# The end of a one-layer encoder step: the last 256 columns of y turned to token rows by TensorE, the upper columns scaled by GpSimd

## The chip, the cores and the metric

The kernel runs on one core of a Trainium2 chip. A core has TensorE (PE, with its weight loads as PEld), VectorE (DVE), ScalarE (ACT), GpSimd (POOL) and SyncE (SP, here only a queue that issues DMAs). The metric is the device time of one launch in microseconds (us); lower is better. The time before is 2154.39 us, the median of three runs from 2150.38 to 2154.47.

## The reference, cut to what matters

The reference is one inference step of a one-layer streaming encoder over 1024 prompt tokens and 64 sample tokens, width 1024: retention and sliding-window attention, a mix, cross attention and a SwiGLU, each added to the residual. Only the last two lines concern the change: the SwiGLU's down projection completes the residual stream, and the final RMSNorm scales every token by its own factor and every feature by a gain.

```python
    return (jax.nn.silu(hn @ w_gate) * (hn @ w_up)) @ w_down
...
    y = xf * lax.rsqrt(jnp.mean(xf * xf, axis=-1, keepdims=True) + EPS)
    if g is not None:
        y = y * g.astype(jnp.float32)
...
    y_prompt = rms_norm(hp, g_final)
    y_sample = rms_norm(hs, g_final)
```

## The kernel before, in words

Activations lie transposed: features on the 128 partitions, the 1088 tokens as columns. The residual y is eight tiles `y[0]` to `y[7]` of 128 features by 1088 columns; in the profile `y[0]` is called `rstd_f`, the others `y`. Matrix products run in a split of each operand into a high and a low part (three matmuls in place of one: `mm3`, lines 157 to 159), and most of the kernel in a Strassen-like scheme (`strassen`, with `multiply` at lines 223, 224 and 226).

The down projection goes over three groups of features of the hidden layer. In the last group the upper half of the columns, 544 to 1087 (`c = 2` below), is completed by the Strassen products, and the function `finish` completes the lower 544 columns by 16 plain products: eight (one for each `y[m]`) for columns 0 to 271 (`c = 0`), then eight for columns 272 to 543 (`c = 1`). A product is nine matmuls. Each is followed by `grow`: VectorE adds the product from PSUM to `y[m]` (line 1746) and ScalarE squares the sum (line 1750). `gather` adds a square to the running sum of squares in `rstd` on VectorE (line 1755).

For each of the three column groups the norm then takes these steps. `sums`: TensorE multiplies 128-token pieces of `rstd` with a matrix of ones, so that token sums land with tokens on partitions (line 1764). `roots`: six small steps give one factor per token (lines 1861 to 1868; the square root on ScalarE, the rest on VectorE). `spread`: TensorE multiplies the factors, broadcast, with the identity, so that each partition holds the factor of every column (line 1782), and ScalarE copies it to `rstd` (line 1786). `scale`: VectorE multiplies `y[m]` by gain and factor in one operation (line 1792) and a DMA stores it; some tiles get the gain by ScalarE (`gain`, line 1797) and the factor by GpSimd (`aside`, line 1805).

PSUM has eight banks, held as four pairs (`bank_pair`, pool `pst` with four buffers). In `finish` the helper `bank` takes a whole pair for each use and leaves its second half idle.

The order on each engine is set by a scheduler of the tile framework, which tracks which instruction reads and writes which tile and puts semaphore waits into the program. `in_order` holds a TensorE step behind the TensorE step before it, and `queued` does the same for VectorE steps in `finish`, so that there the written order stands.

Of the kernel before, what the change touches and what calls it, by code (L numbers as in the profile page):

```python
# [11 lines left out]
F32 = mybir.dt.float32  # L12
F32R = mybir.dt.float32r
AF = mybir.ActivationFunctionType
ALU = mybir.AluOpType
# [4 lines left out]
P = 128  # L20
D = 1024
# [19 lines left out]
HALF = T // 2  # L41
HC = HALF // 2
OPS = ("B11", "T1", "T2", "B21", "T3", "B22", "T4", "B12")

# [65 lines left out]
class Kernel:  # L110
# [1616 lines left out]
    def finish(self, y, rest):  # L1727


        nc = self.nc  # L1730
        tt, stt, ts = nc.vector.tensor_tensor, nc.vector.scalar_tensor_tensor, nc.vector.tensor_scalar
        cols = [slice(0, HC), slice(HC, HALF), slice(HALF, T)]
        squares, factors = {}, {}
        bank = lambda: self.bank_pair()[:, 0, :]

        def product(c, m, q, xs):
            ps = bank()[:, :HC]
            for k, x in enumerate(xs):
                ks = slice(k * P, (k + 1) * P)
                x = x.rearrange("p a (b c) -> p a b c", b=2)[:, :, c]  # L1740
                self.mm3(ps, q[:, 0, ks], q[:, 1, ks], x[:, 0], x[:, 1], k == 0, k == len(xs) - 1)
            return ps

        def grow(c, m, ps):
            v = y[m][:, cols[c]]
            self.queued(lambda: tt(out=v, in0=ps, in1=v, op=ALU.add))
            sq = self.rstd[:, cols[c]]
            if m:
                sq = self.hl.tile([P, HALF], F32, tag="hl", name="sq")[:, :HC]
            nc.scalar.activation(sq, v, AF.Square)  # L1750
            squares[c, m] = sq
# [4 lines left out]

        def sums(c, *more):

            spans = self.spans(cols[c].stop - cols[c].start)
            ps = bank()[:, :2 * len(spans)].rearrange("p (t two) -> p t two", two=2)  # L1760
            parts = [self.rstd[:, cols[c]], *more]
            steps = [(x, i, a, w) for x in parts for i, (a, w) in enumerate(spans)]
            for j, (x, i, a, w) in enumerate(steps):
                self.last_mm = nc.tensor.matmul(ps[:, i, :], x[:, a:a + w], self.ones[:, :2], start=j == 0,  # L1764
                                                stop=j == len(steps) - 1).ins
            r = self.np.tile([P, 5], F32, tag="rf", bufs=2, name="rs_f")[:, :len(spans)]
            factors[c] = r, spans, ps[:, :, 0]

        def roots(c, between=None):
            r, spans, ps = factors[c]  # L1770
            v = self.np.tile([P, 5], F32, tag="vf", bufs=2, name="rf_v")[:, :len(spans)]
            t = self.np.tile([P, 5], F32, tag="tf", bufs=2, name="rf_t")[:, :len(spans)]
            self.steps(r, v, t, ps, between)

        def spread(c, copied=True):
            r, spans, _ = factors[c]
            for part in ((0, 2), (2, 5)) if len(spans) > 4 else ((0, len(spans)),):
                pb = bank()
                a0, a1 = spans[part[0]][0], spans[part[1] - 1][0] + P
                for i in range(*part):  # L1780
                    at = spans[i][0] - a0
                    self.last_mm = nc.tensor.matmul(pb[:, at:at + P], r[:, i:i + 1].broadcast_to([P, P]), self.ident,  # L1782
                                                    start=True, stop=True).ins
                c0 = cols[c].start
                if copied:
                    self.last_copy = nc.scalar.copy(self.rstd[:, c0 + a0:c0 + a1], pb[:, :a1 - a0]).ins
            return pb

        def scale(c, k, by=None, queue=nc.sync):
            o = y[k][:, cols[c]]  # L1790
            by = self.rstd[:, cols[c]] if by is None else by
            self.queued(lambda: stt(o, o, self.gains[:, 3, k:k + 1], by, ALU.mult, ALU.mult))
            queue.dma_start(self.io["o_y"][k, :, cols[c]], o)

        def gain(c, k):
            o = y[k][:, cols[c]]
            nc.scalar.mul(o, o, self.gains[:, 3, k:k + 1])

        def put(c, k, queue=nc.sync):
            queue.dma_start(self.io["o_y"][k, :, cols[c]], y[k][:, cols[c]])  # L1800

        def aside(c, k, queue=None):
            o = y[k][:, cols[c]]
            with self.tc.issue_after(self.last_aside) if self.last_aside else nullcontext():
                self.last_aside = nc.gpsimd.tensor_tensor(out=o, in0=o, in1=self.rstd[:, cols[c]], op=ALU.mult).ins
            if queue:
                put(c, k, queue)

        self.last_aside = None
        left = (5, 6, 7)  # L1810
        spare = (5, 6)
        for j in range(2 * KT):
            c, m = divmod(j, KT)
            ps = self.in_order(lambda: product(c, *rest[m]))
            grow(c, rest[m][0], ps)
            if (j - 1) % KT and j and j < 2 * KT - 1:
                gather((j - 1) // KT, rest[(j - 1) % KT][0])
# [8 lines left out]
            if j == KT + 6:  # L1826
                pb0 = self.in_order(lambda: spread(0))[:, :HC]
                aside(0, KT - 1, nc.sync)
            if c and m in (0, 1, 2, 5, 6):
                scale(2, m if m < 3 else m - 2)  # L1830
            if c and 0 < m < 4:
                gain(2, left[m - 1])
            if c and m == 4:
                gain(0, KT - 1)
        for k in spare:
            gain(1, k)
        for k in range(3):
            scale(0, k, pb0)
        for k in left:
            aside(2, k)  # L1840
        self.in_order(lambda: sums(1, *(squares[1, rest[i][0]] for i in (KT - 2, KT - 1))))
        roots(1, lambda: scale(0, 3, pb0))
        for k in range(4, KT - 1):
            scale(0, k, pb0)
            if k < KT - 2:
                put(2, left[k - 4])
        pb = self.in_order(lambda: spread(1))[:, :HC]
        queues = [nc.sync, nc.scalar]
        for i, k in enumerate((0, 1, 2, 5, 3, 4, 6, 7)):
            if i == 3:  # L1850
                with self.tc.issue_after(self.last_copy):
                    put(2, left[2], nc.scalar)
            if k in spare:
                aside(1, k, queues[i % 2])
            else:
                scale(1, k, pb, queues[i % 2])

# [81 lines left out]
```

## Time and profile before

| what | us |
|---|---|
| runs | 2150.38, 2154.39, 2154.47 |
| span of the profiled execution | 2150.0 |
| TensorE busy | 2130.1 |
| VectorE busy | 1550.7 |
| ScalarE busy | 875.7 |
| GpSimd busy | 536.5 |
| first product of `finish` starts | 2114.70 |
| last product of `finish` ends | 2136.64 |
| last store issued | 2146.17 |

The page gives no time of the profiled execution beside its span; the span lies 0.38 us under the lowest run and 4.39 us under the median. Times in the profile are us from the span's start. Matmuls are pipelined: one of 272 columns is listed with 0.29 us, but starts 0.13 us after the one before it. One fp32 matmul that isn't split by the kernel is listed as two instructions. "DVE rstd_f" and "DVE y" in the chain of waits are VectorE steps that write `y`.

### The profile page before, as it was taken

To read this page: it belongs to the slowest core of one execution; us is meant where nothing else is said; L and a number is where in the kernel's file an instruction comes from. 1 tells how busy PE (TensorE), PEld (TensorE's weight loads), DVE (VectorE), ACT (ScalarE), POOL (GpSimd) and SP (SyncE) were. 2 spreads that over 40 slices of the span, in tenths; PEclk is the share of its full clock that TensorE was granted. 3 is DMA by queue.
4 is the path that set the end of the run, shared out by engine and by line. 5 is a ranking of instruction groups with operands and counts; after the bars stand their busy time and mean duration, and the time that the engine had idled before them with its cause. 6 is when DMAs were issued, how large, how long until landed. Compare 5 with 4: busy or idle time off the path is not lost. (4 is left out here: it accounts for less than half of the span.)

```text
span 2150.0 us, 41711 instructions
## 1 busy us (share of the span) xinstructions
PE 2130.1 (99%) x16377; PEld 2080.0 (97%) x16377; DVE 1550.7 (72%) x2909; ACT 875.7 (41%) x1897; POOL 536.5 (25%) x450
## 2 busy tenths in 40 slices
PE   9999999999999999999999999999999999999998
PEld 9999999999999997889999999999999999999998
DVE  8987979776677568656545555778777777877688
ACT  7343434344434356553233433333222222344344
POOL 0000000012253125540000000015556555514532
PEclk9999999999999999999999999999999999999999
DMA  7344444434345485336443121422342333383442
GB/s 257 126 133 120 129 136 128 139 119 155 121 144 176 159 265 188 116 115 212 137 143 104 40 63 53 155 65 98 121 146 94 106 113 106 103 328 125 141 131 99
DMA packets 169893, 290.85 MB, mean 135 GB/s; under 512 B 39266, under 2 KB 96546, under 8 KB 169698
## 3 DMA queue, kind: packets, MB, share of 16 engines
q1 hardware_dynamic: 161522, 268.74, 38.8%
q0 software_dynamic: 3424, 10.82, 1.4%
q10 hardware_dynamic: 4752, 8.64, 1.1%
q8 instruction: 129, 2.11, 0.4%
q14 instruction: 66, 0.54, 0.1%
HBM read 196.97 MB, written 91.16 MB: 134 GB/s over the span
## 5 line engine op out<-in xcount | busy, mean ns | idle before, releaser
L125 DVE TENSOR_TENSOR wq<-raw,wq 128x512 fp32r<-128x512 f32 (+1 forms) x499 | 429.6, 866 | 145.1 <-ACT wq L124 141.9
L124 ACT CAST wq<-raw 128x512 fp32r<-128x512 f32 (+1 forms) x499 | 301.6, 614 | 556.0 <-PE pq L226 217.8
L224 PE MATMUL pq<-T,wq 128*128 128x272 f32 x1832 | 492.1, 288 | 0.5 <-DVE T L125 0.5
L223 PE MATMUL pq<-T,wq 128*128 128x272 f32 x1832 | 490.2, 287 | 2.0 <-ACT wq L124 1.1
L224 PE MATMUL pq<-B,wq 128*128 128x272 f32 x1592 | 427.2, 288 | 1.0 <-DVE B L125 1.0
L223 PE MATMUL pq<-B,wq 128*128 128x272 f32 x1592 | 425.6, 287 | 0.8 <-ACT B L124 0.8
L226 PE MATMUL pq<-T,wq 128*128 128x272 f32 x1832 | 382.7, 289 | 1.0 <-DVE wq L125 1.0
L201 POOL TENSOR_TENSOR raw<-raw 128x512 f32<-128x512 f32 (+1 forms) x44 | 64.3, 1461 | 1252.2 <-DVE wq L125 569.6
L223 PEld LDWEIGHTS pq<-T,wq 128*128 128x128 f32 x1832 | 344.2, 188 | 3.2 <-ACT xsq L502 1.3
L224 PEld LDWEIGHTS pq<-T,wq 128*128 128x128 f32 x1832 | 344.0, 188 | 1.5 <-issue 0.7
L226 PE MATMUL pq<-B,wq 128*128 128x272 f32 x1592 | 331.9, 289 | 0.0
L224 PEld LDWEIGHTS pq<-B,wq 128*128 128x128 f32 x1592 | 299.0, 188 | 2.4 <-DVE B L125 1.9
L223 PEld LDWEIGHTS pq<-B,wq 128*128 128x128 f32 x1592 | 298.9, 188 | 1.1 <-ACT B L124 1.0
L226 PEld LDWEIGHTS pq<-T,wq 128*128 128x128 f32 x1832 | 289.7, 189 | 2.4 <-DVE wq L125 1.2
L226 PEld LDWEIGHTS pq<-B,wq 128*128 128x128 f32 x1592 | 251.7, 189 | 0.9 <-issue 0.7
L277 DVE TENSOR_TENSOR u<-pq,u 128x544 f32<-128x544 f32 x177 | 127.3, 720 | 69.4 <-PE pq L226 69.0
L616 DVE TENSOR_TENSOR stage<-pq,u 128x544 f32<-128x544 f32 x112 | 80.4, 720 | 32.2 <-PE pq L226 26.0
L157 PE MATMUL pd<-xc,wq 128*128 128x256 f32 (+1 forms) x256 | 74.6, 292 | 0.0
L159 PE MATMUL pd<-xc,wq 128*128 128x256 f32 (+1 forms) x256 | 74.3, 290 | 0.0
L158 PE MATMUL pd<-xc,wq 128*128 128x256 f32 (+1 forms) x256 | 74.1, 290 | 0.0
L1566 POOL TENSOR_TENSOR stage<-stage,rstd_f 128x544 f32<-128x544 f32 x40 | 63.9, 1607 | 39.1 <-ACT stage L1565 39.1
L204 POOL TENSOR_TENSOR raw<-raw 128x512 f32<-128x512 f32 (+1 forms) x44 | 59.4, 1349 | 52.8 <-DVE wq L125 50.3
(388 smaller groups left out, 4515.3 us busy)
## 6 DMA issues: line engine op xcount, KB each, us to landing
hl<-d_op SPq DMA_DIRECT2D x85, 272.0 KB, 5.4
d_qkv<-stage SPq DMA_DIRECT2D x44, 272.0 KB, 2.5
d_op<-stage SPq DMA_DIRECT2D x44, 272.0 KB, 2.4
d_op<-ht SPq DMA_DIRECT2D x44, 272.0 KB, 3.2
raw<-w_gate SPq DMA_DIRECT2D x22, 512.0 KB, 3.5
raw<-w_up SPq DMA_DIRECT2D x22, 512.0 KB, 4.5
raw<-w_down SPq DMA_DIRECT2D x16, 512.0 KB, 4.6
d_gate<-stage ACTq DMA_DIRECT2D x28, 272.0 KB, 2.7
```

Source lines behind the costliest of these rows:

```text
L124: self.last_cast = self.nc.scalar.copy(hi, src).ins
L125: return self.nc.vector.tensor_tensor(out=lo, in0=src, in1=hi.bitcast(F32), op=ALU.subtract).ins
L157: mm(ps, wh, xh, start=start, stop=False)
L158: mm(ps, wh, xl, start=False, stop=False)
L159: self.last_mm = mm(ps, wl, xh, start=False, stop=stop).ins
L201: tt(out=a11, in0=a11, in1=a21, op=sub)
L223: mm(ps[:, c, :HC], w[:, 0, ks], x[:, 0, cs], start=start, stop=False)
L224: mm(ps[:, c, :HC], w[:, 0, ks], x[:, 1, cs], start=False, stop=False)
L226: self.last_mm = mm(ps[:, c, :HC], w[:, 1, ks], x[:, 0, c * HC:(c + 1) * HC], start=False, stop=stop).ins
L277: add = lambda out, a, b: nc.vector.tensor_tensor(out=out, in0=a, in1=b, op=ALU.add)
L616: nc.vector.tensor_tensor(out=o, in0=ps, in1=sb, op=ALU.add)
L1566: nc.gpsimd.tensor_tensor(out=g, in0=g, in1=r[t], op=ALU.mult)
```

## The change: what it does

The lower columns are cut at 288 in place of 272: `c = 0` is columns 0 to 287, `c = 1` columns 288 to 543 (256 of them). The products and their adds are as before, with 288 and 256 columns.

For `c = 1` there is no `spread` and no scaling along columns. TensorE turns 128-token blocks of `y[m]`: `turn` multiplies the block, as the stationary operand, with a diagonal matrix of the gains (`diag`, eight 128x128 pieces that ScalarE makes from the identity), so that tokens come to lie on partitions with the gain already in. Sixteen such fp32 matmuls fill two PSUM pairs. Then the factor is a scalar for each partition, and four operations of 128x512 (two on VectorE, two on ScalarE) write the result, which is stored in a new output `o_yt`, token by token; the host puts it in its place in y. The sums of `c = 1` are taken in four parts, between the turns.

For `c = 2` ScalarE multiplies five tiles by the gain during the first products (or earlier: the scheduler moves four of them ahead), and GpSimd multiplies these five by the factor right after the `spread` that follows product 5; VectorE scales the other three between later products. For `c = 0` two tiles go the same way by GpSimd, and six by VectorE. `sums` and `roots` of `c = 2` come after product 3 in place of product 5, and its `spread` after product 5 in place of product 7.

`bank` now hands out both halves of a PSUM pair before it takes the next pair.

```diff
+CUT = 288
...
-        cols = [slice(0, HC), slice(HC, HALF), slice(HALF, T)]
-        bank = lambda: self.bank_pair()[:, 0, :]
+        cols = [slice(0, CUT), slice(CUT, HALF), slice(HALF, T)]
+        ring, slots = self.slots["T2"]
+        extra = [self.rings[ring].tile(f"last{i}", F32, slot=s).rearrange("p a n -> p (a n)") for i, s in enumerate(slots)]
+        diag = extra[0][:, :KT * P].rearrange("p (k m) -> p k m", m=P)
+        turned = extra[1][:, :2 * D].rearrange("p (i m) -> p i m", i=2)
+
+        def bank():
+            if not banks:
+                pair = self.bank_pair()
+                banks.extend((pair[:, 0, :], pair[:, 1, :]))
+            return banks.pop(0)
...
+        def sums(c, x, start, stop):
+            r, spans, ps = factors[c]
+            for i, (a, w) in enumerate(spans):
+                self.last_mm = nc.tensor.matmul(ps[:, i, :], x[:, a:a + w], self.ones[:, :2], start=start and i == 0,
+                                                stop=stop and i == len(spans) - 1).ins
...
+        def turn(n):
+            m = rest[n][0]
+            for i, pair in enumerate(pairs):
+                a = CUT + i * P
+                self.last_mm = nc.tensor.matmul(pair[:, m // 4, m % 4 * P:(m % 4 + 1) * P], y[m][:, a:a + P], diag[:, m, :],
+                                                start=True, stop=True).ins
...
-        left = (5, 6, 7)
-        spare = (5, 6)
+        by_pool, by_vector = (0, 1, 2, 3, 4), (5, 6, 7)
+        for k in range(KT):
+            nc.scalar.mul(diag[:, k, :], self.ident, g[:, 3, k:k + 1])
         for j in range(2 * KT):
             c, m = divmod(j, KT)
             ps = self.in_order(lambda: product(c, *rest[m]))
             grow(c, rest[m][0], ps)
...
+            if j < len(by_pool):
+                gain(2, by_pool[j])
+            if j == 3:
+                self.in_order(lambda: whole_sums(2))
+                roots(2)
             if j == 5:
-                self.in_order(lambda: sums(2))
-                roots(2)
-            if j == KT - 1:
                 self.in_order(lambda: spread(2))
-            if j == KT + 3:
-                self.in_order(lambda: sums(0))
+                for k in by_pool:
+                    aside(2, k)
+            if j in (6, 7, 9):
+                scale(2, by_vector[(6, 7, 9).index(j)])
+            if j == KT + 2:
+                self.in_order(lambda: whole_sums(0))
                 roots(0)
...
+        for n in range(6):
+            self.in_order(lambda: turn(n))
+        last_sums(0, self.rstd[:, cols[1]])
+        last_sums(1, squares[1, rest[5][0]])
+        last_sums(2, squares[1, rest[6][0]])
+        self.in_order(lambda: turn(6))
+        last_sums(3, squares[1, rest[7][0]])
+        self.in_order(lambda: turn(7))
+        scale(0, 5)
+        scale(0, 6)
+        roots(1, lambda: scale(0, 7))
+        r = factors[1][0]
+        for i in range(2):
+            for h in range(2):
+                o, ps = turned[:, i, h * 512:(h + 1) * 512], pairs[i][:, h, :]
+                if h:
+                    nc.scalar.mul(o, ps, r[:, i:i + 1])
+                else:
+                    self.queued(lambda: ts(o, ps, r[:, i:i + 1], None, ALU.mult))
+                (nc.scalar if h else nc.sync).dma_start(self.io["o_yt"][i * P:(i + 1) * P, h * 512:(h + 1) * 512], o)
```

Outside `finish` the order of the instructions stays, but for the gains and diagonals that ScalarE takes in between earlier steps, and for a few VectorE steps just ahead of the first product. Three places inside it follow. In the changed program all line numbers are higher by one up to `finish`, and differ from there on.

TensorE, from product 0 to product 1; `pq_` with a number is a PSUM pair, `B21` and `T4` are the operands of even and odd products, `wb` the weights; the semaphores that a row waits for stand behind it. Before:

```order
L159 MATMUL pq_24742<-B21_24272,wb_24730 128x272
L157 MATMUL pq_24754<-T4_24285,wb_24730 128x272 [waits DVE_49]
L159 MATMUL pq_24754<-T4_24286,wb_24730 128x272
L157 MATMUL pq_24767<-B21_24271,wb_24733 128x272 [waits DVE_49,PE_49,Activation_49]
L157 MATMUL pq_24781<-T4_24285,wb_24733 128x272 [waits DVE_49]
```

So each product wrote to a pair of its own. With the change, and with the sums of `c = 2` (L1776) behind product 3:

```order
L160 MATMUL pq_24752<-B21_24272,wb_24730 128x288
L158 MATMUL pq_24752<-T4_24285,wb_24730 128x288 [waits DVE_49]
L160 MATMUL pq_24752<-T4_24286,wb_24730 128x288
L158 MATMUL pq_24778<-B21_24271,wb_24733 128x288 [waits PE_49,Activation_49]
L158 MATMUL pq_24778<-T4_24285,wb_24733 128x288 [waits DVE_49]
L1776 MATMUL pq_24807<-ones_64,rstd_68 128x2 [waits PE_49]
L158 MATMUL pq_24807<-B21_24271,wb_24736 128x288 [waits DVE_49,Activation_49]
```

Now products 0 and 1 share pair 24752, 2 and 3 share 24778, the sums and product 4 share 24807. The count of VectorE steps that the second user of a pair waits for is in the built program, and is this: product 1 before waited for the VectorE step `u5<-pq_24660` of the Strassen scheme; now it waits for the step `rstd_f<-pq_24752`, which is the add of product 0, the reader of the pair's other half. Product 3 waits in the same way for the add of product 2, product 4 for the first step of `roots`, product 8 for the add of product 7, product 10 for that of 9, product 11 for the first step of `roots` of `c = 0`, its `spread` for the add of product 12, and product 14 for the add of product 13.

VectorE, from the add of product 6 on; `y0_22086` is `y[5]`, `y1_22087` is `y[6]`, `y2_22088` is `y[7]`, `rstd_f` is `y[0]`. Before:

```order
L1746 TENSOR_TENSOR y1_22087<-pq_24838,y1_22087 128x272
L1755 TENSOR_TENSOR rstd_68<-rstd_68,sq_24820 128x272
L1746 TENSOR_TENSOR y2_22088<-pq_24852,y2_22088 128x272
L1755 TENSOR_TENSOR rstd_68<-rstd_68,sq_24849 128x272
L1746 TENSOR_TENSOR rstd_f_15865<-pq_24875,rstd_f_15865 128x272
```

The adds and the gathers alternated there, with no `scale` before the add of product 8. With the change:

```order
L1756 TENSOR_TENSOR y1_22087<-pq_24853,y1_22087 128x288
L1765 TENSOR_TENSOR rstd_68<-rstd_68,sq_24847 128x288
L1806 SCALAR_TENSOR_TENSOR y0_22086<-y0_22086,gains_65,rstd_68 128x544
L1756 TENSOR_TENSOR y2_22088<-pq_24883,y2_22088 128x288
L1765 TENSOR_TENSOR rstd_68<-rstd_68,sq_24878 128x288
L1806 SCALAR_TENSOR_TENSOR y1_22087<-y1_22087,gains_65,rstd_68 128x544
L1756 TENSOR_TENSOR rstd_f_15865<-pq_24883,rstd_f_15865 128x256
```

A `scale` of 544 columns now stands ahead of the adds of products 7 and 8.

GpSimd, its last steps. Before:

```order
L1805 TENSOR_TENSOR y2_22088<-y2_22088,rstd_68 128x272
L1805 TENSOR_TENSOR y0_22086<-y0_22086,rstd_68 128x544
L1805 TENSOR_TENSOR y1_22087<-y1_22087,rstd_68 128x544
L1805 TENSOR_TENSOR y2_22088<-y2_22088,rstd_68 128x544
L1805 TENSOR_TENSOR y0_22086<-y0_22086,rstd_68 128x272
L1805 TENSOR_TENSOR y1_22087<-y1_22087,rstd_68 128x272
```

All six stood at the end, none ahead of product 14. With the change:

```order
L1816 TENSOR_TENSOR rstd_f_15865<-rstd_f_15865,rstd_68 128x544
L1816 TENSOR_TENSOR y0_22084<-y0_22084,rstd_68 128x544 x2
L1816 TENSOR_TENSOR y1_22085<-y1_22085,rstd_68 128x544 x2
L1816 TENSOR_TENSOR rstd_f_15865<-rstd_f_15865,rstd_68 128x288
L1816 TENSOR_TENSOR y0_22084<-y0_22084,rstd_68 128x288
```

Each row marked x2 is two tiles. The first five instructions now stand behind the `spread` that follows product 5, the last two behind the `spread` that follows product 12.

More of the change, by code (lines that the diff above doesn't have):

```diff
@@ L1755, in gather, with begin_sums, whole_sums @@
             self.queued(lambda: tt(out=acc, in0=acc, in1=squares[c, m], op=ALU.add))
-        def sums(c, *more):
-            spans = self.spans(cols[c].stop - cols[c].start)
+        def begin_sums(c):
+            spans = self.spans(width(c))
             ps = bank()[:, :2 * len(spans)].rearrange("p (t two) -> p t two", two=2)
[L1761 to L1765, printed above, removed]
-            r = self.np.tile([P, 5], F32, tag="rf", bufs=2, name="rs_f")[:, :len(spans)]
-            factors[c] = r, spans, ps[:, :, 0]
+            r = self.np.tile([P, 5], F32, tag="rf", bufs=2, name="rs_f")[:, :len(spans)]
+            factors[c] = r, spans, ps
+        def sums(c, x, start, stop):
[3 more added lines that the diff above has]
+                                                stop=stop and i == len(spans) - 1).ins
+        def whole_sums(c):
+            begin_sums(c)
+            sums(c, self.rstd[:, cols[c]], True, True)
         def roots(c, between=None):
@@ L1772, in roots, with spread @@
             t = self.np.tile([P, 5], F32, tag="tf", bufs=2, name="rf_t")[:, :len(spans)]
-            self.steps(r, v, t, ps, between)
-        def spread(c, copied=True):
+            self.steps(r, v, t, ps[:, :, 0], between)
+        def spread(c):
             r, spans, _ = factors[c]
@@ L1784, in spread, with put, scale, aside @@
                 c0 = cols[c].start
[L1785 to L1789, printed above, removed]
+                nc.scalar.copy(self.rstd[:, c0 + a0:c0 + a1], pb[:, :a1 - a0])
+        def put(c, k):
+            nc.sync.dma_start(self.io["o_y"][k, :, cols[c]], y[k][:, cols[c]])
+        def scale(c, k):
             o = y[k][:, cols[c]]
-            by = self.rstd[:, cols[c]] if by is None else by
-            self.queued(lambda: stt(o, o, self.gains[:, 3, k:k + 1], by, ALU.mult, ALU.mult))
-            queue.dma_start(self.io["o_y"][k, :, cols[c]], o)
+            self.queued(lambda: stt(o, o, g[:, 3, k:k + 1], self.rstd[:, cols[c]], ALU.mult, ALU.mult))
+            put(c, k)
         def gain(c, k):
             o = y[k][:, cols[c]]
[L1797 to L1802, printed above, removed]
+            nc.scalar.mul(o, o, g[:, 3, k:k + 1])
+        def aside(c, k):
             o = y[k][:, cols[c]]
@@ L1835, in finish @@
[L1835 to L1848, printed above, removed]
@@ new lines, in finish, with last_sums @@
+            if j in (KT + 2, KT + 3):
+                gain(0, j - KT - 2)
+            if j == KT + 4:
+                self.in_order(lambda: spread(0))
+                for k in range(2):
+                    aside(0, k)
+            if j > KT + 4:
+                scale(0, j - KT - 3)
+        pairs = [self.bank_pair() for i in range(2)]
+        begin_sums(1)
+        def last_sums(n, x):
+            self.in_order(lambda: sums(1, x, n == 0, n == 3))
+        for n in range(6):
+            self.in_order(lambda: turn(n))
```

40 lines of the change are left out of this document (12 added, 28 removed).

## The prediction

> **What bounds the kernel now.** I read the page first, then the chain of waits for the end, then the rows of each engine in the stretch that the diff touches, then that stretch in windows.
>
> ```profile
> span 2150.0 us, 41711 instructions
> PE 2130.1 (99%) x16377; PEld 2080.0 (97%) x16377; DVE 1550.7 (72%) x2909; ACT 875.7 (41%) x1897; POOL 536.5 (25%) x450
> 2114.70:2136.60 21.90, 21.90 (x180) 21.80 (x179) 19.84 (x51) 11.06 (x27) 0.58 (x1) 1.00 0.12 47
> ```
>
> TensorE bounds the program. The last row is the stretch of the sixteen products: its columns are the length, then busy time of PE, PEld, DVE, ACT and POOL, the granted clock, DMA share and GB/s. TensorE has no gap there, at full clock, so whatever stops it there is paid in full. VectorE is busy 19.84 of 21.90: the average hides that it is nearly full as well, so an add that stands behind other VectorE work is late. GpSimd does almost nothing there.
>
> The tail, in the chain of waits (start, length, step):
>
> ```profile
> 2136.64 1.92 PE pq L1764 x18
> 2138.58 0.16 DVE rf_v L1861
> ...
> 2139.26 0.64 DVE rf_t L1866
> 2139.93 1.26 DVE rf_t L1867
> 2141.22 0.17 DVE rs_f L1868
> 2141.43 1.67 PE pq L1782 x6
> 2143.12 0.39 ACT rstd L1786
> ...
> 2144.44 1.63 DVE y L1792 x4
> ```
>
> After the last product come sums, roots, spread, copy and scaling, one after the other, to 2146.07: 9.43 from 2136.64. From there to the span's end are 3.93 for the last store. This chain is what the diff shortens.
>
> **The tail, part by part.** For `c = 1` the spread (1.67) and copy (0.39) go, and the scaling becomes two steps on each of two engines. Sixteen turns come in, each listed as two matmuls. Next are rows of the timeline (start, length, engine, line, step) and, last, a group (count, busy time, mean ns of one).
>
> ```profile
> 2121.50 1.17 PE L1764 MATMUL pq<-ones,rstd 128*128 128x2 f32 x10
> 2122.53 0.37 PE L157 MATMUL pq<-B,wb 128*128 128x272 f32 x1
> 2124.89 1.38 PE L1782 MATMUL pq<-ident,rs_f 128*128 128x128 f32 x10
> 2126.03 0.37 PE L157 MATMUL pq<-B,wb 128*128 128x272 f32 x1
> 2123.62 0.16 DVE L1861 TENSOR_SCALAR rf_v<-pq 128x5 f32<-128x5 f32 x1
> 2124.67 0.17 DVE L1868 SCALAR_TENSOR_TENSOR rs_f<-rf_t,rs_f 128x5 f32<-128x5 f32 x1
> L1797 ACT ACTIVATE y<-y,gains 128x544 f32<-128x544 f32 x2 | 1.5, 738 | 0.0
> ```
>
> From one kind's first start to the next kind's, ten sums matmuls take 1.03 and ten 128x128 ones 1.14, so a turn is 2 x 0.114 = 0.23. Sixteen turns are 3.65 and the eight last sums (two spans, four parts, two instructions each) 16 x 0.103 = 1.65. All but the last two turns stand ahead of the roots: 5.3 - 0.46 = 4.84. Roots that nothing disturbs take 2124.84 - 2123.62 = 1.22. Then ScalarE does two steps of 512 columns, by its 544-column row at most 0.74 each, 1.48, with a store's issue between, for which I allow 0.4. Together 7.9 in place of 9.43: 1.5 gained. The last store is now 256 KB where 136 KB stood; at 361 GB/s (row of 2146 below) that is 0.35 more, and the four stores come at once, for which I take as much again. The gain on the tail is 0 (all of it lost to the stores) to 1.5; I take **-0.8**. The cut at 288 costs nothing: 288 and 256 add up to 2 x 272. The diagonals and gains lie on ScalarE, busy 11.06 of 21.90; without that cover a gain would make a square 0.74 late.
>
> **The products.** The price lies here. In the changed program two products share a PSUM pair, and the second waits for the add of the first. Whether that costs anything depends on when the add is done.
>
> ```profile
> 2114.70 0.29 PE L157 MATMUL pq<-B,wb 128*128 128x272 f32 x1
> 2115.83 0.29 PE L157 MATMUL pq<-T,wb 128*128 128x272 f32 x1
> ...
> 2118.02 0.43 DVE L1746 TENSOR_TENSOR rstd_f<-pq,rstd_f 128x272 f32<-128x272 f32 x1
> 2118.37 0.72 DVE L1648 TENSOR_TENSOR y<-u,y 128x544 f32<-128x544 f32 x1
> 2119.00 0.79 DVE L1746 TENSOR_TENSOR y<-pq,y 128x272 f32<-128x272 f32 x2
> 2119.70 1.55 DVE L1660 TENSOR_TENSOR rstd<-rstd,sq 128x544 f32<-128x544 f32 x2
> ```
>
> A product takes 1.13, so 1.20 with 288 columns and 1.06 with 256. Product 0 ends at 2115.9, but its add starts at 2118.02, behind Strassen steps that the change doesn't touch, and ends near 2118.47. Before, product 1 started regardless. Now it starts at 2118.5: **2.6** idle. I follow the chain on:
>
> - Products 1 and 2 run to 2120.9. VectorE does the 544-column step and the two of L1660 (0.63 and 1.46 from start to start), then add 1, and add 2 to 2121.4. Product 3, which waits for it, loses **0.5**.
> - Product 3 ends at 2122.65, the sums at 2123.7; product 4 waits for the first step of the roots: **0.3**.
> - The spread waits for add 5 and product 6 for a copy: **0.5**. Product 7 ends near 2130.4.
> - Products 8 and 10 wait for adds 7 and 9, and ahead of these stand gathers and a `scale` each, while GpSimd works through five 544-column steps. For that, these rows:
>
> ```profile
> 2076.13 1.38 POOL L202 TENSOR_TENSOR raw<-raw 128x384 f32<-128x384 f32 x1
> 2076.63 1.29 DVE L125 TENSOR_TENSOR wq<-raw,wq 128x384 fp32r<-128x384 f32 x1
> 2139.83 1.33 POOL L1805 TENSOR_TENSOR y<-y,rstd 128x544 f32<-128x544 f32 x1
> L1755 DVE TENSOR_TENSOR rstd<-rstd,sq 128x272 f32<-128x272 f32 x12 | 5.2, 434 | 0.0
> L1792 DVE SCALAR_TENSOR_TENSOR y<-y,gains,rstd 128x544 f32<-128x544 f32 x4 | 3.1, 781 | 0.0
> ```
>
> In the tail's chain above a step of five columns, L1867, takes 1.26, just while GpSimd's 1.33 runs; with GpSimd idle the like L1868 takes 0.17. At 2076 a 384-column step on VectorE takes 1.29 and ends when GpSimd's step does. So a VectorE step with its inputs in SBUF waits for a whole GpSimd step, and gets its turn between two. Gather and `scale` are such steps; the adds, which read PSUM, went on. With GpSimd starting at 2127.9, its second step ends at 2130.6; gather to 2131.0; third step to 2132.35; `scale` to 2133.1; add 7 to 2133.55. Product 8 starts at 2133.6 in place of 2130.4: **3.2**. Products 8 and 9 end at 2135.7; the next gather and `scale` fall behind the fourth and fifth step (to 2136.95), then add 8, a gather, add 9 to 2138.1: product 10 loses **2.4**.
>
> - Product 11 waits for the first root of `c = 0`: **0.4**. The spread of `c = 0` waits for add 12 and product 14 for add 13, each an add of 0.43 and two hand-overs: **0.6** and **0.6**.
>
> Sum: 2.6 + 0.5 + 0.3 + 0.5 + 3.2 + 2.4 + 0.4 + 0.6 + 0.6 = **11.1**. If VectorE and GpSimd don't take turns, the terms 3.2 and 2.4 become 0.8 (gather, `scale`, add after add 6) and 0.5: 6.8. These are the bounds for the pairs.
>
> The stores of the five GpSimd tiles now go out during the products, where the DMA share was 0.12, so nothing waits for them.
>
> **The clock.** TensorE hasn't been idle beside products before, so the trace shows only the tail:
>
> ```profile
> 2136.00:2138.00 2.00, 2.00 (x21) 2.00 (x19) 2.00 (x5) 1.22 (x3) 1.99 (x2) 1.00 0.36 139
> 2138.00:2140.00 2.00, 0.54 (x5) 0.45 (x5) 1.69 (x6) 0.21 (x1) 2.00 (x3) 1.00 0.87 307
> 2140.00:2142.00 2.00, 0.57 (x2) 0.57 (x3) 1.97 (x4) 0.00 (x0) 1.16 (x1) 0.68 0.98 345
> 2142.00:2144.00 2.00, 1.08 (x6) 0.79 (x4) 1.06 (x4) 0.39 (x1) 0.42 (x1) 0.50 0.89 313
> 2146.00:2148.00 2.00, 0.00 (x0) 0.00 (x0) 0.08 (x1) 0.00 (x0) 0.00 (x0) 0.50 1.01 361
> ```
>
> TensorE stops at 2138.55, and the mean clock of 0.68 from 2140 to 2142 means full speed for 0.72 and half speed after: the drop came 2.2 after the stop. Idles of 2.6, 3.2 and 2.4 are of that size. A drop makes a product 1.06 to 1.2 longer; no row shows how soon the clock returns. One slow product after each of the three would be 3.4, and four in all 4.5; none is the other end. Behind products 8 and 9 VectorE is late anyway and covers what they lose. I take **+1.5** (0 to 4.5).
>
> The Trainium skill, "TensorE: Matmul & The Clock Gate", Part 1, says that the clock halves after at least one whole idle window of about 3.4 us, free-running. By that the drop after 2.2 could not have come, unless the rest of its window counted as idle, so here the trace speaks against the strict reading; by that rule none of my idles would halve the clock, this term would be 0, and the result 1.5 lower.
>
> **Sum.** 11.1 + 1.5 - 0.8 = +11.8 on the profiled span: 2161.8. That execution's span lies 4.39 under the median; the same offset gives **2166.2 us**. Its own range: clock and store terms 0 to 4.5 and -1.5 to 0, and 1.5 either way on the lock's turns: 2162 to 2171.
>
> **Rivals.**
>
> *The halves hold nothing back (not slower).* The mechanism: a product waits only on the PSUM half that it writes, or the add of the other half is always done. Then all idles are 0 and the tail's gain remains: 2154.4 - 0.8 = 2153.6. It decides from the point where the idles together stay under 0.8. For it: by product 8 VectorE had caught up and waited 1.21 for it, as the bracket of this row says.
>
> ```profile
> 2127.44 0.44 DVE L1746 TENSOR_TENSOR rstd_f<-pq,rstd_f 128x272 f32<-128x272 f32 x1 [1.21 <-PE pq L159]
> ```
>
> Against it: the row at 2118.02 alone gives 2.6, and the wait is in the program. Chance 0.07.
> The Trainium skill, "PSUM — Partial Sum Buffer", Summary, lets an engine read one bank while matmuls write another, so the chip would allow this; the wait is the program's, and no run here shows it absent.
>
> *No turns between GpSimd and VectorE.* Adds are late only by their own queue: 6.8 - 0.8 and no clock loss, +6.0: 2160.4. For it: GpSimd's first steps may come later than I have them, or fall beside adds. Against it: the 1.26 for five columns. Chance 0.17.
>
> *The clock stays at half through the products.* After the first idle the remaining 20.8 of the stretch take twice as long, and the later idles vanish because adds catch up: 2.6 + 20.8 - 0.8 = +22.6, so 2177. For it: at half clock nothing in the tail brought it back up to the span's end. Against it: there TensorE had almost nothing to do. Chance 0.05.
>
> **Chances.** The forecast has 0.68, the rest 0.03 is anything else. The likeliest is 2166.2. The range 2158 to 2171 takes in the forecast and the second rival with 2 below it, and leaves out the first, the third and the edges. A measurement of this kernel tells 0.2%, 4.3 us, from no change: all cases but the first are slower by more than that. Faster 0.02 (the first rival with a larger gain than I can work out), same 0.09 (the first rival, and a small second one), slower 0.89.
>
> **What would show it.** In the changed profile: idle of TensorE just ahead of product 1, 8 and 10, put down to VectorE's adds, of some 2.6, 3.2 and 2.4; gathers or scales on VectorE stretched to over 1 us beside GpSimd's 1.33; a granted clock under 1.00 in windows of the products; and a tail of 8 from the last product to the last scaling. Wrong would be a stretch of products that still takes 22, or a gap ahead of product 1 that isn't there; if gaps 8 and 10 are below 1, the second rival holds.

## The result, and the profile after

The changed kernel took 2164.1 us, the median of five runs from 2160.7 to 2165.29, against 2150.38 us for the kernel before (five runs, 2149.48 to 2154.47). The ratio is 1.0057, with a 95% interval of 1.0045 to 1.007: it is slower, by 12 us by the ratio (the two medians lie 13.7 apart). The prediction was 2166.2 with a range of 2158 to 2171. The page of the profiled execution begins:

```profile
span 2159.3 us, 41753 instructions
PE 2136.5 (99%) x16401; PEld 2086.5 (97%) x16401; DVE 1548.3 (72%) x2901; ACT 880.1 (41%) x1907; POOL 538.0 (25%) x451
```

The shares of the engines hardly differ from before; the difference shows in the end of the program. Profiles also differ by up to some microseconds ahead of that, where the order of the instructions hardly changes: product 0 starts at 2111.55 here and at 2114.70 before. So from here on the end is counted from the start of product 0, and cut where TensorE turns from products to the last sums (before) or to the first turn (now). These are the two stretches, of the kernel before (first two rows) and of the changed one; the columns are those of the prediction's rows.

```profile
2114.70:2136.47 21.77, 21.77 (x178) 21.67 (x177) 19.71 (x51) 10.93 (x27) 0.46 (x1) 1.00 0.12 45
2136.47:2150.00 13.53, 3.72 (x26) 3.34 (x24) 8.32 (x20) 1.38 (x4) 6.17 (x6) 0.66 0.73 258
```

```profile
2111.55:2147.03 35.48, 26.99 (x178) 25.26 (x177) 24.84 (x50) 10.75 (x26) 9.03 (x7) 0.90 0.19 73
2147.03:2159.30 12.27, 5.52 (x50) 5.33 (x48) 4.26 (x12) 2.03 (x5) 0.00 (x0) 0.75 0.44 154
```

The products take 13.71 us more (35.48 against 21.77), the tail 1.26 less (12.27 against 13.53). TensorE, which had no gap there, is idle for 8.5 of the 35.48, and its granted clock is 0.90 in place of 1.00.

TensorE's rows after a gap, from the timeline (start, length, step; in brackets the idle time and what ended it). In this kernel L1756 is the add, L1765 the gather, L1806 the scale on VectorE, L1816 GpSimd's, L1776 the sums, L1796 the spread, L1889 the first step of the roots.

```profile
2115.57 0.50 PE L158 MATMUL pq<-T,wb 128*128 128x288 f32 x1 [2.66 <-DVE rstd_f L1756]
...
2120.30 0.40 PE L158 MATMUL pq<-T,wb 128*128 128x288 f32 x1 [0.55 <-DVE y L1756]
...
2123.11 0.37 PE L158 MATMUL pq<-B,wb 128*128 128x288 f32 x1 [0.35 <-DVE rf_v L1889]
...
2132.68 0.52 PE L158 MATMUL pq<-B,wb 128*128 128x256 f32 x1 [2.97 <-DVE y L1756]
...
2137.12 0.38 PE L158 MATMUL pq<-B,wb 128*128 128x256 f32 x1 [0.52 <-DVE y L1756]
...
2139.36 0.39 PE L158 MATMUL pq<-T,wb 128*128 128x256 f32 x1 [0.36 <-DVE rf_v L1889]
...
2142.27 0.93 PE L1796 MATMUL pq<-ident,rs_f 128*128 128x128 f32 x6 [0.52 <-DVE y L1756]
...
2144.78 0.39 PE L158 MATMUL pq<-B,wb 128*128 128x256 f32 x1 [0.52 <-DVE y L1756]
```

In order these are products 1, 3, 4, 8, 10 and 11, the spread of `c = 0`, and product 14: each the second user of a PSUM pair, each ended by a VectorE step that reads the pair's other half.

VectorE and GpSimd ahead of products 8 and 10 (the last row of VectorE is the add of product 9, for which product 10 waits):

```profile
2129.01 1.49 DVE L1765 TENSOR_TENSOR rstd<-rstd,sq 128x288 f32<-128x288 f32 x1
2130.42 1.85 DVE L1806 SCALAR_TENSOR_TENSOR y<-y,gains,rstd 128x544 f32<-128x544 f32 x1
2132.19 0.44 DVE L1756 TENSOR_TENSOR y<-pq,y 128x288 f32<-128x288 f32 x1
2132.55 1.22 DVE L1765 TENSOR_TENSOR rstd<-rstd,sq 128x288 f32<-128x288 f32 x1
2133.70 1.87 DVE L1806 SCALAR_TENSOR_TENSOR y<-y,gains,rstd 128x544 f32<-128x544 f32 x1
...
2136.64 0.42 DVE L1756 TENSOR_TENSOR y<-pq,y 128x256 f32<-128x256 f32 x1 [0.37 <-PE pq L160]
```

```profile
2128.83 6.16 POOL L1816 TENSOR_TENSOR y<-y,rstd 128x544 f32<-128x544 f32 x4
```

A gather is listed with 1.49 and 1.22 in place of 0.43, a scale with 1.85 and 1.87 in place of 0.78, and GpSimd's four steps take 1.54 on the mean in place of 1.33: the two engines take turns. The add between them at 2132.19, which reads PSUM, takes its usual 0.44.

The granted clock (the last column but two) in windows of 2 us:

```profile
2114.00:2116.00 2.00, 0.43 (x2) 0.44 (x3) 2.00 (x4) 0.82 (x2) 0.00 (x0) 0.93 0.00 0
2116.00:2118.00 2.00, 2.00 (x10) 2.00 (x9) 1.50 (x3) 1.25 (x3) 0.00 (x0) 0.50 0.00 0
2118.00:2120.00 2.00, 1.75 (x9) 1.51 (x8) 0.67 (x2) 0.98 (x2) 0.00 (x0) 0.72 0.00 0
...
2132.00:2134.00 2.00, 1.31 (x6) 1.32 (x7) 2.00 (x4) 0.44 (x1) 2.00 (x2) 0.70 0.44 168
2134.00:2136.00 2.00, 2.00 (x12) 2.00 (x11) 2.00 (x3) 0.07 (x1) 0.99 (x1) 0.50 0.64 250
2136.00:2138.00 2.00, 1.48 (x11) 1.28 (x11) 1.38 (x3) 0.77 (x2) 0.00 (x0) 0.95 0.72 279
```

Behind each of the two long gaps the clock is at half for a while, and the two products that follow run in it.

The tail, in the chain of waits:

```profile
2147.20 2.68 PE pq L1823 x24
2149.87 1.24 PE pq L1776 x12
...
2152.04 0.16 DVE rf_v L1889
...
2153.39 0.76 DVE last L1883
2154.18 1.34 ACT last L1881 x2
```

The first root comes 4.84 after the start of this chain, no root step is stretched any more (GpSimd is done by then), and the last scaling ends at 2155.52, 8.5 after the first turn.

### The profile page after: what moved, and what is told of

Its sections match the earlier page's. It is cut to its first block, busy times and chain, and to the rows that moved or that the text cites. A ratio compares the mean times of both kernels' runs of the same rounds, so it can differ in the third digit from the quotient of the medians.

```text
span 2159.3 us, 41753 instructions
## 1 busy us (share of the span) xinstructions
PE 2136.5 (99%) x16401; PEld 2086.5 (97%) x16401; DVE 1548.3 (72%) x2901; ACT 880.1 (41%) x1907; POOL 538.0 (25%) x451
## 4 chain that ended last, share of the span: by engine, by line
PE 89%; DVE 6%; DMA 2%; ACT 1%; issue 1%; POOL 0%; SPq 0%; DVEq 0%; POOLq 0%; ACTq 0%
PE pq L227 17%; PE pq L225 17%; PE pq L224 17%; PE pd L158 8%; PE pd L159 8%; PE pd L160 8%; DVE wq L126 1%; PE pss L1009 1%; PE pout L1079 1%; DMA hl<-d_op 1%; DVE T L126 1%; PE pk L770 1%; PE pp L1055 1%; DVE B L126 1%; PE po L158 1%
```

## The experiments

All kernels were timed beside the kernel before, and their ends were cut in the same way. The table gives the stretches of one profile each; the rows behind it follow with each experiment. In e2, e3 and e5 a part of the output lacks its factor, because GpSimd's multiplications are left out.

| kernel | products | tail | end | ratio to before, 95% interval |
|---|---|---|---|---|
| before | 21.77 | 13.53 | 35.30 | |
| the change | 35.48 | 12.27 | 47.75 | 1.0057 (1.0045 to 1.007) |
| the change, again | 35.18 | 12.29 | 47.47 | 1.0070 (1.0046 to 1.0095) |
| e4: before, pairs shared | 34.70 | 12.52 | 47.22 | 1.0050 (1.0033 to 1.0066) |
| e1: own pairs | 32.04 | 12.33 | 44.37 | 1.0062 (1.0041 to 1.0083) |
| e2: no GpSimd work | 34.33 | 12.31 | 46.64 | 1.0065 (1.0050 to 1.0080) |
| e3: own pairs, no GpSimd work | 26.40 | 12.33 | 38.73 | 1.0035 (1.0022 to 1.0048) |
| e5: e3 with late sums | 22.67 | 12.37 | 35.04 | 0.9998 (0.9989 to 1.0007) |
| e6: e5 with GpSimd's work | 26.45 | 12.34 | 38.79 | 1.0014 (1.0005 to 1.0023) |
| e7: gaps filled | 33.60 | 12.34 | 45.94 | 1.0074 (1.0053 to 1.0094) |
| b1 | 21.72 | 13.57 | 35.29 | 1.0004 (0.9996 to 1.0013) |
| b2 | 22.86 | 13.05 | 35.91 | 1.0007 (0.9998 to 1.0016) |

The times don't follow the ends everywhere. By its median e1 is 12.2 slower than the kernel before and e3 7.1, where their ends say 9.1 and 3.4; the others agree to 2.4. What lies ahead of product 0 differs from profile to profile by more than that (it starts at 2116.83 in e1, at 2111.55 in the change), and no experiment says why. So differences of 1 to 4 us between the ends are read from rows, and the times alone would not show that e1 gains anything over the change.

The theory going in was the prediction's: shared pairs hold the products, GpSimd's turns with VectorE lengthen two of the gaps, the clock adds to it. The main rival was that GpSimd's work alone is the cost.

**e4: the sharing alone, in the kernel before.**

```diff
-        bank = lambda: self.bank_pair()[:, 0, :]
+        banks = []
+
+        def bank():
+            if not banks:
+                pair = self.bank_pair()
+                banks.extend((pair[:, 0, :], pair[:, 1, :]))
+            return banks.pop(0)
```

> The kernel before, with one edit: both halves of a PSUM pair are handed out, as in the change. Theory: a gap of about 2.7 us ahead of product 1, about 0.5 us ahead of every later second user of a pair, and a stretch at half clock after the first gap (1.5 to 2 us): end 41 to 44 us against 35.3, 0.25 to 0.4% slower than before. Rival (halves cost nothing, the change's other parts do): end 35 to 36 us.

```profile
2115.71 0.59 PE L157 MATMUL pq<-T,wb 128*128 128x272 f32 x1 [2.53 <-DVE rstd_f L1752]
2120.26 0.39 PE L157 MATMUL pq<-T,wb 128*128 128x272 f32 x1 [0.53 <-DVE y L1752]
2123.31 0.39 PE L157 MATMUL pq<-T,wb 128*128 128x272 f32 x1 [0.53 <-DVE y L1752]
2126.06 0.56 PE L157 MATMUL pq<-B,wb 128*128 128x272 f32 x1 [0.35 <-DVE rf_v L1867]
```

The end is 47.22, nearly as long as with the whole change: those few lines suffice to make the products 12.9 longer. The early gaps are as expected; the end is 3 to 6 longer than expected. Two things are seen that the expectation didn't have: the clock fell twice (the second time ahead of the fourth row, behind short gaps and the sums), and three of the later gaps were 0.8 to 0.9. The rival, that halves cost nothing, falls.

**e1: the change with own pairs.**

```diff
         def bank():
-            if not banks:
-                pair = self.bank_pair()
-                banks.extend((pair[:, 0, :], pair[:, 1, :]))
-            return banks.pop(0)
+            return self.bank_pair()[:, 0, :]
```

> The change, but every use of PSUM in the end takes a whole pair, as before; all else as in the change. The end is counted from the start of product 0 to the end of the span: 35.3 before, 47.75 with the change. Theory (the shared pairs hold the products): no gap of TensorE over 0.3 us ahead of products 1, 3, 8, 10, 14, granted clock 1.00 over the products, end 34 to 36.5 us, time within 0.1% of before. Rival (GpSimd's turns with VectorE are the cost, wherever the pairs are): VectorE stays 3 to 4 us late from add 7 on, TensorE waits for it four products later, end 38 to 42 us.

Rows of the timeline (in e1 and the kernels after it, but for e2 and e7, the sums are L1773, the gather L1762, the scale L1803):

```profile
2123.66 1.28 PE L1773 MATMUL pq<-ones,rstd 128*128 128x2 f32 x10 [1.89 <-DVE rstd L1661]
...
2137.64 1.25 DVE L1762 TENSOR_TENSOR rstd<-rstd,sq 128x288 f32<-128x288 f32 x1
2138.94 1.35 PE L1773 MATMUL pq<-ones,rstd 128*128 128x2 f32 x6 [3.25 <-DVE rstd L1762]
```

The gaps ahead of products 1, 3, 8, 10 and 14 are gone, as the theory has it, but the end is 44.37, not 36.5: two other gaps have opened, and half clock behind each. The second, ahead of the sums of `c = 0`, ends with a gather (the middle row) that is stretched to 1.25 beside GpSimd, behind two scales of 1.88 and 1.85: the rival's cost, which is thus real too. The first is one that neither theory had: the sums of `c = 2`, which the change moved from behind product 5 to behind product 3, wait for the last sum of squares of the upper half (L1661), with which VectorE is late.

**e2 and e3: GpSimd's multiplications left out, with shared and with own pairs.**

```diff
             o = y[k][:, cols[c]]
-            with self.tc.issue_after(self.last_aside) if self.last_aside else nullcontext():
-                self.last_aside = nc.gpsimd.tensor_tensor(out=o, in0=o, in1=self.rstd[:, cols[c]], op=ALU.mult).ins
             put(c, k)
```

> The change, with GpSimd's multiplications by the factor left out (the seven tiles are stored without it, so that part of the output lacks the factor); pairs shared as in the change. Theory (pairs, and GpSimd's turns as a second cost that acts through them): the gap ahead of product 8 falls from 2.97 to about 0.8 us, products 8 and 9 run at full clock, the gaps ahead of 1, 3, 10, 14 stay at 2.66, 0.55, 0.5, 0.5: end 43 to 45 us, 3 to 4.5 us less than the change. Rival (GpSimd's turns are the whole cost): end 35 to 37 us. Rival (GpSimd costs nothing): end 47 to 48 us.

```profile
2119.17 0.40 PE L158 MATMUL pq<-T,wb 128*128 128x288 f32 x1 [3.65 <-DVE rstd_f L1756]
...
2135.68 0.38 PE L158 MATMUL pq<-B,wb 128*128 128x256 f32 x1 [0.86 <-DVE y L1756]
```

By its rows e2 says what was expected: the gap ahead of product 8 is 0.86 and products 8 and 9 run at full clock. By its end, 46.64, it missed: VectorE was a microsecond later at product 1 (3.65), and a second stretch at half clock came behind product 4. That GpSimd is the whole cost is refuted; the end of this single profile can't price its share, since the fall of the clock behind product 4 came with it.

> Both: a whole pair for every use, and GpSimd's multiplications left out (part of the output lacks the factor). Theory: what is left of the change is its tail; end 34.0 to 34.8 us, 0.5 to 1.3 us less than before, no gap over 0.3 us. If it is over 36 us, there is a third cost that neither the pairs nor GpSimd make.

```profile
2123.51 1.28 PE L1773 MATMUL pq<-ones,rstd 128*128 128x2 f32 x10 [2.38 <-DVE rstd L1661]
```

```profile
2121.92 1.54 DVE L1661 TENSOR_TENSOR rstd<-rstd,sq 128x544 f32<-128x544 f32 x2
```

The end is 38.73, over the 36 that was set as the sign of a third cost, and its one long gap is again the early sums: 2.38, ended by the two steps of L1661. In the changed kernel this wait lies inside the gap of 2.66 ahead of product 1 and can't be seen.

**e5 and e6: the sums back in their place, without and with GpSimd's work.** Both have own pairs. The spread of `c = 2` and VectorE's three scales move back with the sums.

```diff
...
-            if j == 3:
+            if j == 5:
                 self.in_order(lambda: whole_sums(2))
                 roots(2)
-            if j == 5:
+            if j == 7:
                 self.in_order(lambda: spread(2))
...
-            if j in (6, 7, 9):
-                scale(2, by_vector[(6, 7, 9).index(j)])
+            if j in (8, 9, 11):
+                scale(2, by_vector[(8, 9, 11).index(j)])
```

> As e3 (own pairs, GpSimd's multiplications left out, so part of the output lacks the factor), and the sums and roots of c = 2 go back behind product 5, its spread behind product 7, VectorE's three scales behind products 8, 9 and 11. Theory (the third cost is the early sums, which wait for the squares of the upper half that VectorE is late with): the gap of 2.38 us ahead of the sums goes, and with it the stretch at half clock behind it; end 34.2 to 35.0 us (38.7 in e3, 35.3 before), which leaves the new tail alone: 0.3 to 1.1 us gained. Rival (own pairs still hold the products somewhere, or the tail is dearer): end over 36 us.

```profile
2118.27 0.40 PE L158 MATMUL pq<-T,wb 128*128 128x288 f32 x1 [0.25 <-DVE y L1647]
```

The gap ahead of the sums is gone, the row above is TensorE's only one with idle time ahead of it, and the clock is 1.00 in every window of the products. The end is 35.04, 3.7 less than e3 and just over the upper edge of what was expected. The gap of 0.25 that remained is ended by a Strassen step of VectorE. So the third cost was the early sums with the half clock behind them.

> As e5, but with GpSimd's seven multiplications in: the five of 544 columns start behind the spread after product 7. Theory (a VectorE step between two SBUF operands waits for a whole GpSimd step): gathers and scales of 1.2 to 1.9 us, the sums of c = 0 wait 2 to 4 us, one stretch at half clock behind that; end 39 to 42 us. Rival (GpSimd was dear only because the early sums had made VectorE late): end 34 to 36 us.

Rows of e6 (L1893 is the last step of the roots):

```profile
2128.16 1.88 DVE L1803 SCALAR_TENSOR_TENSOR y<-y,gains,rstd 128x544 f32<-128x544 f32 x1
2130.29 1.55 DVE L1803 SCALAR_TENSOR_TENSOR y<-y,gains,rstd 128x544 f32<-128x544 f32 x1
2132.10 1.22 DVE L1762 TENSOR_TENSOR rstd<-rstd,sq 128x256 f32<-128x256 f32 x1
```

```profile
2127.87 6.65 POOL L1813 TENSOR_TENSOR y<-y,rstd 128x544 f32<-128x544 f32 x4
```

```profile
2134.98 0.96 PE L1793 MATMUL pq<-ident,rs_f 128*128 128x128 f32 x6 [2.99 <-DVE rs_f L1893]
```

The end is 38.79 (39 to 42 expected): VectorE falls behind by its turns with GpSimd, the roots of `c = 0` come late, and TensorE stands for 2.99 ahead of that spread (I had expected it at the sums before), with half clock behind. Against e5, which leaves this work out, it costs 3.75 (3.1 between the medians). It was dear by itself, not only because the early sums had made VectorE late.

**e7: the gaps filled with spare matmuls.** The change, with the waits as they are; TensorE is only kept at work.

```diff
+        def fill(r, n):
+            m, q, xs = r
+            spare = self.bank_pair()[:, 0, :CUT]
+            for i in range(n):
+                self.last_mm = nc.tensor.matmul(spare, q[:, 0, :P], xs[0][:, 0, cols[0]], start=i == 0, stop=i == n - 1).ins
...
             ps = self.in_order(lambda: product(c, *rest[m]))
+            if j in (0, 7):
+                self.in_order(lambda: fill(rest[m], 16 if j == 0 else 22))
```

> The change, with spare matmuls that nobody reads put into TensorE's two long gaps: 16 of 288 columns behind product 0 and 22 behind product 7, into a PSUM pair of their own. They shorten no wait, they only keep TensorE at work. Theory (the gaps cost twice, once as idle time and once because the clock granted falls to half behind them): granted clock 1.00 through products 1, 2, 8 and 9; products 1 and 2 take 2.4 us in place of 3.9; what 8 and 9 gain is partly lost again as a longer gap ahead of product 10; from product 0 to the first turn 33.0 to 34.2 us in place of 35.5. Rival (the clock falls by the clock's own rhythm or by the waits, whatever TensorE does): 35 to 36 us.

```profile
2114.75 2.27 PE L1758 MATMUL pq<-B,wb 128*128 128x288 f32 x16
2117.57 0.40 PE L158 MATMUL pq<-T,wb 128*128 128x288 f32 x1 [0.54 <-DVE rstd_f L1762]
...
2130.02 3.06 PE L1758 MATMUL pq<-T,wb 128*128 128x288 f32 x22
...
2137.22 0.39 PE L158 MATMUL pq<-B,wb 128*128 128x256 f32 x1 [1.61 <-DVE y L1762]
```

```profile
2118.00:2120.00 2.00, 2.00 (x17) 2.00 (x15) 1.87 (x4) 1.26 (x3) 0.00 (x0) 1.00 0.00 0
...
2134.00:2136.00 2.00, 1.61 (x14) 1.40 (x12) 2.00 (x2) 0.00 (x0) 1.54 (x1) 1.00 0.89 347
```

The clock stays at 1.00 in every window of the products, which take 33.60, 1.9 less than in the change: that is what the clock costs, net. The gap ahead of product 10 grows from 0.52 to 1.61, as expected: slow products had covered it. The times, whose spread is some microseconds, don't show 1.9.

**b1 and b2: a version to beat both.** Own pairs, the loop of the kernel before, the change's tail; all of `c = 2` on VectorE, of which three tiles while TensorE turns; GpSimd keeps two tiles of 288 columns.

```diff
...
-            if j == 3:
+            if j == 5:
                 self.in_order(lambda: whole_sums(2))
                 roots(2)
-            if j == 5:
+            if j == KT - 1:
                 self.in_order(lambda: spread(2))
-                for k in by_pool:
-                    aside(2, k)
-            if j in (6, 7, 9):
-                scale(2, by_vector[(6, 7, 9).index(j)])
...
+            if c and m in (0, 1, 2, 5, 6):
+                scale(2, m if m < 3 else m - 2)
...
-        scale(0, 5)
-        scale(0, 6)
-        roots(1, lambda: scale(0, 7))
+        for k in (5, 6, 7):
+            scale(2, k)
+        for k in range(2, KT - 1):
+            scale(0, k)
+        roots(1, lambda: scale(0, KT - 1))
```

> A version to beat both: own pairs, the loop of the kernel before (sums of c = 2 after product 5, spread after 7, five scales on VectorE), the change's tail with turns, and the three scales left of c = 2 on VectorE while TensorE turns; GpSimd only takes two tiles of 288 columns at the end. Theory: no gap over 0.3 us in the products, granted clock 1.00, end 34.3 to 35.3 us: 0 to 1 us less than before, less than a time of this kernel can tell (ratio 0.9995 to 1.0000). If VectorE's eight scales at the end hold the roots: end 35.5 to 36.5 us.

```profile
2140.57 4.86 DVE L1803 SCALAR_TENSOR_TENSOR y<-y,gains,rstd 128x544 f32<-128x544 f32 x8
```

```profile
2148.00:2150.00 2.00, 0.00 (x0) 0.00 (x0) 0.10 (x1) 0.82 (x2) 0.00 (x0) 0.63 1.03 366
```

The products take 21.72, as before, with no gap. But the tail is 13.57 and not 12.3: eight scales (the first row gives the form of the first; three have 544 columns, five 288) and their stores crowd into it, and the DMA engines are full (1.03 of their time, 366 GB/s) while the last steps end. The end is that of before, and the ratio says the same.

b2 has the spread of `c = 2` one product earlier and one scale more behind product 7. Against b1:

```diff
...
-            if j == KT - 1:
+            if j == KT - 2:
                 self.in_order(lambda: spread(2))
+            if j == KT - 1:
+                scale(2, 7)
...
-        for k in (5, 6, 7):
+        for k in (5, 6):
             scale(2, k)
```

> As b1, but the spread of c = 2 stands behind product 6 and a sixth scale of c = 2 behind product 7, in the 1.08 us in which VectorE waited in b1, so that one store of 278 KB fewer is left for the end. Theory (b1 lost the tail's gain to its stores): the stretch stays at 21.7 to 22.0 us, the tail falls from 13.6 to 12.6 to 13.0, end 34.4 to 35.0 us against 35.3, too little for a time to tell (ratio 0.9990 to 1.0005). Rival (the roots come too late for the spread): TensorE waits 0.3 us or more ahead of the spread, end 35.3 us or more.

```profile
2129.56 1.38 PE L1793 MATMUL pq<-ident,rs_f 128*128 128x128 f32 x10 [0.92 <-DVE rs_f L1891]
```

The rival holds: the roots come too late for the earlier spread, TensorE stands for 0.92. The tail is 0.5 shorter, the end 35.91, longer than before. No version here beats the kernel before by anything that could be measured.

**The change once more.**

> The changed kernel once more, on the same chip as the three others. Theory: end 47 to 49 us with the same gaps ahead of products 1, 3, 8, 10, 14 as in the first profile to 0.3 us, but for the first, which hangs on how late VectorE is and may be 2.5 to 3.7 us.

Its end is 47.47, with gaps of 2.67, 0.55, 0.35, 3.00, 0.52, 0.36, 0.52 and 0.52: the first profile was no chance.

## Why the prediction was right, point by point

- **The pairs.** The gaps came at the places named. Predicted and measured: product 1 2.6 and 2.66, product 3 0.5 and 0.55, product 4 0.3 and 0.35, product 8 3.2 and 2.97, product 11 0.4 and 0.36, spread of `c = 0` and product 14 0.6 each and 0.52 each. For product 6 0.5 was predicted; it starts 0.33 late, 1.47 after the spread's start (2125.60 to 2127.07) in place of 1.14. e4 shows the cause by itself, e1 shows these gaps gone with own pairs. These are the idle times of the brackets; what a wait costs is a little more (see the sum below).
- **Product 10: mis-sized.** Predicted 2.4, measured 0.52; with the clock held up (e7) 1.61. There are two reasons. At half clock products 8 and 9 took up most of VectorE's delay themselves, and in the change the last step, the add at 2136.64, even waited 0.37 for product 9. So the 4.44 from the start of product 8 to that of product 10 is not VectorE's chain. In e7, where these products ran at full clock and that add waited for nothing, it was 4.03 (2133.19 to 2137.22), where the prediction's numbers give 4.5 (2138.1 - 2133.6): VectorE's chain was half a microsecond shorter than predicted.
- **The turns between GpSimd and VectorE.** Right, and shown by e2 (gap 8 falls to 0.86; 0.8 was predicted for that case) and by e6 against e5 (3.75 us). Two readings in the argument for them were inexact. The step at 2076.63 does not end when GpSimd's does but 0.41 later (2077.92 against 2077.51), as a step would that starts when GpSimd's ends; and the L1867 that took 1.26 works on three columns, not five.
- **The clock: mis-sized.** The term was +1.5 (0 to 4.5). From their first matmul to their last, products 1 and 2 took 3.89 (2115.57 to 2119.46) in place of 17 x 0.133 = 2.26, products 8 and 9 3.64 in place of 2.0: +3.3. By e7 only 1.9 of this counts: from product 1 to product 3 it takes 3.23 in place of 4.73, but from product 8 to product 10 4.03 in place of 4.44, because VectorE is late there anyway, as the prediction has it. Its reading that a fall comes some 2.2 after TensorE stops was wrong in kind: in these runs the falls come on a grid (last section). The strict reading of the Trainium skill, "TensorE: Matmul & The Clock Gate", Part 1, that a whole idle window is needed, fails here: idle times of 2.66 and 2.97, shorter than its window of about 3.4, were followed by half clock. That the total by that reading, 2164.7, comes out nearer to the measured time is luck.
- **The tail.** Predicted 0.8 less, measured 1.26, with two errors that offset each other. From the first turn to the last scaling it takes 8.5 where 7.9 was predicted; from there to the span's end 3.78, 0.15 less than the 3.93 before, where 0.7 more was allowed for the stores. The DMA engines are busy for 0.44 of the tail in place of 0.73, and the stores of `c = 2` lie earlier, so that allowance was too large. How much of the 1.26 belongs to the turns is not shown: e4, with the old tail behind products that wait, also came down to 12.52, and b1, with the new tail behind products that don't, took 13.57.
- **The sum.** Predicted +11.8 on the span and the end; measured +12.45 on the end (47.75 against 35.30): products +13.71 for 11.1 + 1.5, tail -1.26 for -0.8. The idle times of the brackets add up to 8.8, with 0.33 ahead of product 6. But the prediction counted from the pace of one product to the start of the next, and so counted, from start to start less the usual distance, the waits take 10.4: a matmul is listed with 0.29 while the next one usually starts 0.13 after it, a difference that a bracket leaves out, and the second matmul behind most gaps starts 0.1 late. With 3.3 of half clock this makes 13.7, all that the products grew. So the pairs' term was 0.7 too large (product 10's 2.4 stands for 0.8, most of the others are a little too small) and the clock's 1.8 too small: errors of both signs met.
- **The time.** 2166.2 against 2164.1 looks better than it is. The growth between the medians is 13.7, 1.9 more than predicted, and the base was 4.0 too high: 2154.39 was the median of three runs, over five it is 2150.38. The 4.39 that was added to the span was the distance to that median; every run on record has a time only 1.7 to 1.9 over its own span (2161.16 and 2159.3 for the profile here).
- **What it didn't see.** The early sums of `c = 2` were priced at 0.3, for the first step of the roots. With own pairs they cost 2.38 and the half clock behind (e3 against e5: 3.7). They made no error in the total because with shared pairs the gap ahead of product 1 gives VectorE the time to catch up: there L1661 is done at 2117.6, long ahead of the sums at 2121.59. For the same reason the costs don't add: by the ends of single profiles, own pairs alone take 3.4 off, leaving out GpSimd alone 1.1, both together 9.0.
- **The rivals.** That the halves hold nothing back, that there are no turns, and that the clock stays at half through all products: refuted by the rows of the changed kernel (a gap of 2.66, a scale of 1.85, a clock back at 1.00 at 2119.12).

## What to carry to other kernels

Two users of one tracked buffer are one user to the scheduler: handing out the other half of a PSUM pair, which looks like more depth, makes the next product wait for the last one's reader, and how much that costs is read from how late that reader is. A step handed to GpSimd can hold VectorE for longer (1.33) than VectorE would need for it (0.78), so where VectorE is nearly full the hand-over can be a loss even if GpSimd is idle: e6, with seven tiles on GpSimd, ends at 38.79, b1, with five of them back on VectorE and in other places, at 35.29. And when several causes make the same engine late, undo them one at a time and all together, because the first wait hides the others.

## What the runs showed of the hardware

Half clock came in pieces of one length. From the mean clocks in the windows of 2 us of the change, it fell at 2115.72 (0.93 in the window from 2114) and rose at 2119.12 (0.72 from 2118), fell at 2132.80 and rose at 2136.20: 3.40 each time. The two falls are 17.08 apart, five times 3.42, and the fall at the program's end (0.82 from 2152, so 2153.28) comes 37.56 behind the first, eleven times 3.41. In the second profile of the change the first piece was 3.40 again (0.74 from 2116 and 0.91 from 2120 give 2116.96 and 2120.36). So a fall costs a whole piece, and it comes on a grid that doesn't start with the gap; this agrees with the free-running window of about 3.4 that the Trainium skill, "TensorE: Matmul & The Clock Gate", Part 1, states.

It can also cost two. In e1, behind the gap of 3.25, it fell at 2139.08 (0.77 from 2138) and rose only at 2145.88 (0.53 from 2144), 6.80 later, though TensorE had no gap in between; the first 1.2 of these were sums with two columns each.

How little work in a piece makes the clock fall stays open: in e4 it fell near 2125.9 after gaps of only 0.53 and 0.35 and the sums of two columns each, in e2 at 2126.60 after 0.55, 0.35 and the same sums; in e7 a gap of 1.61 left it at 1.00. That matmuls of two columns count for little would fit all of these, but no run tests it.
